# A decoder layer on one core: mLSTM queries and keys projected with stationary activations and turned by VectorE and moves, FOX columns as one run of seven groups

## The chip, the core and the metric

The kernel runs on one core of a Trainium2 chip. The metric is the device time of one launch in microseconds (us). Before the change it was 1252.22 us, the median of three runs between 1251.11 and 1255.26.

TensorE (PE) multiplies a stationary operand of up to 128 rows x 128 columns with a moving operand of up to 128 x 512 and accumulates into banks of 128 x 512 float32. VectorE (DVE) and ScalarE (ACT) evict and prepare, GpSimd (POOL) and SyncE (SP) issue transfers. Each engine works through its own queue in order.

## The reference, cut to what matters

One layer, batch 1, 256 tokens (S), model width 2048, in float32:

```python
h = rms_norm(x, mix_norm_g)
z = h @ w_in                    # 2048 x 7184: mq mk mv mo mi mf fq fk fv ff
ha = mlstm(mq, mk, mv, mi, mf)  # 4 heads of 256, then per-head norm, * sigmoid(mo)
hb = forgetting_attention(rms_norm(fq), rms_norm(fk), fv, log_sigmoid(ff))  # 8 heads of 128
x = x + concat([ha, hb]) @ w_out
x = x + (gelu(conv3(a)) * g) @ w_down      # a, g = split(rms_norm(x) @ w_up), width 5632
x = x + sigmoid(rms_norm(x) @ w_ple_gate) * (p @ w_ple_proj)
```

The change concerns the second line: the order in which the columns of `z` are computed, and for `mq` and `mk` which operand is stationary.

## The kernel before, in words

**Precision.** A float32 product is made of three: each operand is split into `hi`, its rounding to fp32r, and `lo`, the rest, and hi x hi, hi x lo and lo x hi are added. ACT casts `hi` (L282) and DVE subtracts `lo` (L284) for each block of weights.

**The stream.** `run_stream` walks a list of blocks. A block is one DMA of weights of up to 128 x 1024 elements, issued by SP (L267) three blocks ahead, its split on ACT and DVE also up to three blocks ahead (`AHEAD_SPLIT`), and a function that issues its matmuls on PE. After each block, `pull(2)` takes two steps from `side`, a queue of generators: norms, gates, attention heads, mLSTM scores. Steps are taken alternately from the first two jobs of the queue; those behind wait. `since(n, start)` lets a job wait until n blocks have passed. The framework orders the instructions of each engine by a schedule of its own that follows this order as priority, gives tiles of one tag their buffers, and sets the semaphores.

**Two kinds of groups.** `token_group` (L294 to L320) keeps the activations stationary: for each of 16 k tiles and each of two row tiles of 128 tokens it issues three matmuls with n weight columns moving (L313, L314, L315) into one bank per row tile. Its output has tokens on partitions. With n = 512, a block holds two k tiles, and so it does for each n down to 342. `wide_group` (L323 to L351) keeps the weights stationary: for each k tile and each of four column blocks of 128 it issues one matmul with 512 moving columns (`hi` and `lo` of the activations side by side, L345) and one with 256 (L346) into four banks. Its output is already transposed, with features on partitions; `merge` (L353) adds the two halves of a bank.

**The order of w_in.** FOX keys (2 groups of 512), FOX queries with the mLSTM gates (3 of 344), FOX values with the forget gates (3 of 344), then mLSTM queries and keys as two wide groups each, then values and output gate (2 token groups of 512 each), then `w_out`. The first group also loads and transposes `x` (`load_x`, `prep_x`).

**Squares.** Where token-major columns are needed as feature-major, `square` (L193) lets DVE transpose 32x32 squares, and `move` (L199) lets POOL issue 16 DMAs that put the squares into their places. The FOX queries and keys of each pair of heads go this way (`qk_squares`, tiles `qky` and `qkz`); a head then scales its part with an ACT operation (L567). The residual after `w_out` (`x2y`, `x2z`) and the up projection (`EZ`, `Y`) do the same.

**mLSTM queries and keys.** `qk_group` evicts each bank of a wide group with `merge` into `mqT` or `mkT` (ACT L354, DVE L355) and multiplies each pair by the row of 1/rms (`r1["b"]`, L628), which `rstd_rows` (L157) made with a PE transpose (L160), a copy and two DMAs. `mlstm_scores` multiplies `mkT` with `mqT` (L655, L658) once all FOX heads are taken; `mlstm_out` follows the second group of values, `mlstm_gate` the output gate.

**Buffers.** The token-major columns of FOX and mLSTM (`zbuf`) share three buffers of one tag. The transposed activations `hT`, `catT` (the mixers' outputs), `x2T`, `uA` and `x3T` are pairs of tiles (`Tiles`): 12 k tiles under the tag `aTa`, 4 under `aTb`, two buffers each. In the down projection (`run_units`) six blocks of `aTa` serve as extra `hi`, `lo` and sums (`w2`).

Of the kernel before, what the change touches and what calls it, by code (L numbers as in the profile page):

```python
# [9 lines left out]
F32 = mybir.dt.float32  # L10
F32R = mybir.dt.float32r
# [4 lines left out]
P = 128  # L16
S = 256
# [12 lines left out]
C_FK, C_FV = 5128, 6152  # L30
GATED = 1032
# [12 lines left out]
FRONT = 12  # L44
# [4 lines left out]
def layer_kernel(  # L49
# [19 lines left out]
    def bank(tag, name):  # L69
        return ps.tile([P, 512], F32, tag=tag, name=name)  # L70
# [85 lines left out]

    def rstd_rows(r, pool_):  # L157

        bk = bank("aux", "rstdT")
        pe.transpose(bk[:NT, :P], r, ident)  # L160
        rT = sm.tile([NT, P], F32, tag="rT", name="rT")
        dve.tensor_copy(rT, bk[:NT, :P])
        d = kp.tile([1, S], F32, tag="rstd", name="rstdd", bufs=2)
        pool.dma_start(out=d[0].rearrange("(t p) -> t p", p=P), in_=rT)
        rb = pool_.tile([P, S], F32, name="rb")
        pool.dma_start(out=rb, in_=d.broadcast_to([P, S]))
        return rb
# [155 lines left out]
    def wide_group(w, c0, actT, finish, tag, hold=0):  # L323

        st = {}
        parts = []
        blocks = []
        for k0 in range(0, KD, 2):  # L330
            def fn(hi, lo, k0=k0):
                if k0 == 0:
                    st["b"] = [bank(tag, f"wg{j}") for j in range(4)]
                parts.append((k0, hi, lo))
                if KD - 2 * (hold + 1) <= k0 < KD - 2:
                    return
                for j in range(4):
                    o = st["b"][j]
                    cols = slice(j * P, (j + 1) * P)
                    for kk, h, l in parts:  # L340
                        for i in range(2):
                            a = actT()[:, kk + i, :]
                            first = kk == 0 and i == 0
                            last = kk == KD - 2 and i == 1
                            pe.matmul(o, h[:, i, cols], a, start=first, stop=False)  # L345
                            pe.matmul(o[:, 256:512], l[:, i, cols], a[:, 0:256], start=False, stop=last)  # L346
                    if k0 == KD - 2:
                        finish(j, o)
                parts.clear()
            blocks.append((wsrc(w, k0, 2, c0, 512), fn, None, None, LO_SHIFT))  # L350
        return blocks  # L351

    def merge(dst, b):  # L353
        act.copy(dst, b[:, 256:512])  # L354
        dve.tensor_add(dst, b[:, 0:256], dst)  # L355

    class Tiles:


        def __init__(self, name):  # L360
            self.a = apool.tile([P, FRONT, 512], F32R, tag="aTa", name=name, bufs=2)
            self.b = apool.tile([P, KD - FRONT, 512], F32R, tag="aTb", name=name + "b", bufs=2)

        def __getitem__(self, idx):
            k = idx[1]
            if isinstance(k, slice):
                v, o = (self.a, 0) if k.stop <= FRONT else (self.b, FRONT)
                k = slice(k.start - o, k.stop - o)
            else:
                v, o = (self.a, 0) if k < FRONT else (self.b, FRONT)  # L370
                k -= o
            return v[(idx[0], k, *idx[2:])]

    def new_aT(name):
        return Tiles(name)
# [4 lines left out]
    with mixers:  # L380
# [16 lines left out]
        catT = new_aT("catT")  # L397
# [155 lines left out]
        taken = set()  # L553

        def fox_heads():
            def gen(heads):
                while "em" not in g:
                    yield
                zv = z["fv"]
                scale = FD ** -0.5  # L560
                for h in heads:
# [50 lines left out]
                    split_T(catT[:, 8 + h, :], ob[:, 0:256])  # L612
                    yield
# [5 lines left out]
        mqT = mp.tile([P, 8, S], F32, name="mqT")  # L619
        mkT = mp.tile([P, 8, S], F32, name="mkT")  # L620

        def qk_group(dstT, grp):
            def f(j, b):
                d = dstT[:, grp * 4 + j]
                merge(d, b)
                if j % 2 == 1:
                    d = dstT[:, grp * 4 + j - 1 : grp * 4 + j + 1]
                    dve.tensor_mul(d, d, r1["b"].unsqueeze(1).broadcast_to([P, 2, S]))  # L628
            return f

        WT = {}

        def mlstm_scores():
            def gen():
                while len(taken) < FH:
                    yield
# [4 lines left out]
                for h in range(MH):  # L641
# [12 lines left out]
                    for i in range(2):  # L654
                        pe.matmul(sb[:, 0:256], mkT[:, 2 * h + i, 0:128], mqT[:, 2 * h + i, :],  # L655
                                  start=i == 0, stop=i == 1)
                    for i in range(2):
                        pe.matmul(sb[:, 256:384], mkT[:, 2 * h + i, 128:256], mqT[:, 2 * h + i, 128:256],  # L658
                                  start=i == 0, stop=i == 1)
# [91 lines left out]

        for c in range(2):
            f = evac(get("fk"), c * 512, 512)
            kw = dict(prep=prep_x, load=load_x) if c == 0 else {}
            add(C_FK + c * 512, 512, after(f, lambda: fox_norm("fk", 0)) if c == 1 else f, **kw)
        for c in range(3):
            f = evac(get("fq"), c * 344, 344)
            add(C_MI + c * 344, 344, after(f, lambda: fox_norm("fq", 8)) if c == 2 else f)
        for c in range(3):
            f = evac(get("fv"), c * 344, 344)  # L760
            add(C_FV + c * 344, 344, after(f, gate_math, fox_heads) if c == 2 else f)
        for c in range(2):
            blocks.extend(wide_group(w_in, C_MQ + c * 512, lambda: hT, qk_group(mqT, c), "mm", 1))
        for c in range(2):
            f = qk_group(mkT, c)
            if c == 1:
                f = lambda j, b, f=f: (f(j, b), j == 3 and mlstm_scores())
            blocks.extend(wide_group(w_in, C_MK + c * 512, lambda: hT, f, "mm", 1))
# [48 lines left out]
    with tc.tile_pool(name="ffn", bufs=1) as fp:  # L817
# [98 lines left out]
        def new_raw(j, name):  # L916
# [58 lines left out]
        def run_units(us, first_late, gate):  # L975
            loaded = split = 0
            for i, u in enumerate(us):
                if i == first_late:
                    v = apool.tile([P, 6, BLK], F32R, tag="aTa", name="w2", bufs=2)
                    room.update(late=2, pT=1, e0=1, e1=1, ring=1)  # L980
                    late.update(gate=gate, free=i + LAST_UP + 1, hi=v[:, 0:2], lo=v[:, 2:4],
                                S=v[:, 4:6].rearrange("p b (i c) -> p b i c", c=256))
# [340 lines left out]
```

## Time and profile before

| what | value |
|---|---|
| median of three runs | 1252.22 us |
| the profiled execution | 1252.8 us |
| its span | 1251.1 us |
| granted PE clock, mean | 0.998 |
| PE, DVE, ACT, POOL busy | 1242.3, 829.6, 684.1, 211.4 us |
| w_in stage: wide groups | 147 to 249 us |

The profiled execution is one launch taken by the hardware profiler; its span runs from its first to its last instruction, and the 1.7 us around it belong to the launch. PE rows are matmuls, PEld rows the loads of the stationary operand, which overlap them. A record's line number (L345) is that of the kernel above; names are the program's tiles. A wait is put down to what came last.

### The profile page before, as it was taken

To read this page: it belongs to the slowest core of one execution; us is meant where nothing else is said; L and a number is where in the kernel's file an instruction comes from. 1 tells how busy PE (TensorE), PEld (TensorE's weight loads), DVE (VectorE), ACT (ScalarE), POOL (GpSimd) and SP (SyncE) were. 2 spreads that over 40 slices of the span, in tenths; PEclk is the share of its full clock that TensorE was granted. 3 is DMA by queue.
4 is the path that set the end of the run, shared out by engine and by line. 5 is a ranking of instruction groups with operands and counts; after the bars stand their busy time and mean duration, and the time that the engine had idled before them with its cause. 6 is when DMAs were issued, how large, how long until landed. Compare 5 with 4: busy or idle time off the path is not lost.

```text
span 1251.1 us, 16509 instructions
## 1 busy us (share of the span) xinstructions
PE 1242.3 (99%) x5890; PEld 1051.7 (84%) x5890; DVE 829.6 (66%) x1049; ACT 684.1 (55%) x962; POOL 211.4 (17%) x395
## 2 busy tenths in 40 slices
PE   8999999999999999999999999999999999999998
PEld 7899988888888888888888888888887888888887
DVE  5455567754565654765776676567669998898553
ACT  7655545645554454655565565556556555566542
POOL 2003034200304302112202211220220000050000
PEclk9999999999999999999999999999999999999999
DMA  8667776756667757678777867877798885786560
GB/s 249 175 191 194 217 210 187 207 152 173 197 187 213 224 188 216 207 227 240 229 227 216 252 219 222 242 233 228 221 293 278 283 288 194 261 263 230 174 217 35
DMA packets 133332, 270.74 MB, mean 216 GB/s; under 512 B 13991, under 2 KB 28961, under 8 KB 133249
## 3 DMA queue, kind: packets, MB, share of 16 engines
q1 hardware_dynamic: 119792, 245.99, 63.9%
q0 software_dynamic: 13072, 23.53, 6.6%
q8 instruction: 46, 0.75, 0.2%
q14 instruction: 37, 0.30, 0.1%
q10 hardware_dynamic: 385, 0.16, 0.0%
HBM read 246.02 MB, written 6.83 MB: 202 GB/s over the span
## 4 chain that ended last, share of the span: by engine, by line
PE 95%; DMA 2%; DVE 1%; ACT 1%; issue 0%; POOL 0%; SPq 0%; DVEq 0%; ACTq 0%; POOLq 0%
PE up L1257 13%; PE up L1256 13%; PE up L1258 13%; PE tg L314 10%; PE tg L313 10%; PE tg L315 10%; PE wg L345 5%; PE wg L346 2%; PE dnP L1018 1%; PE dnP L1019 1%; DMA EZ<-Y 1%; PE dnP L1017 1%; PE dn(0, 1)_8857 L1018 1%; PE dn(1, 0)_8861 L1019 1%; PE dn(1, 0)_8861 L1018 1%; PE dn(0, 1)_8857 L1017 1%
## 5 line engine op out<-in xcount | busy, mean ns | idle before, releaser
L970 DVE TENSOR_TENSOR lo<-raw,hi 128x1024 fp32r<-128x1024 f32 x222 | 271.0, 1222 | 177.4 <-ACT hi L969 177.0
L969 ACT CAST hi<-raw 128x1024 fp32r<-128x1024 f32 x222 | 233.2, 1051 | 250.0 <-DMA raw<-in_w_up_dram 102.3
L284 DVE TENSOR_TENSOR lo<-raw,hi 128x1024 fp32r<-128x1024 f32 (+2 forms) x161 | 178.8, 1116 | 148.9 <-ACT hi L282 148.6
L282 ACT CAST hi<-raw 128x1024 fp32r<-128x1024 f32 (+2 forms) x161 | 153.6, 960 | 149.3 <-PE tg L315 81.9
L1258 PE MATMUL up<-hi,x2T 128*128 128x512 f32 x528 | 205.5, 389 | 0.0
L1257 PE MATMUL up<-lo,x2T 128*128 128x512 f32 x528 | 205.4, 389 | 0.0
L1256 PE MATMUL up<-hi,x2T 128*128 128x512 f32 x528 | 204.8, 389 | 0.0
L199 POOL DMA_DIRECT2D EZ<-Y x176 | 93.1, 535 | 175.7 <-DVE Y L193 145.5
L1256 PEld LDWEIGHTS up<-hi,x2T 128*128 128x128 f32 x528 | 99.1, 188 | 20.6
L1257 PEld LDWEIGHTS up<-lo,x2T 128*128 128x128 f32 x528 | 99.1, 188 | 20.5
L1258 PEld LDWEIGHTS up<-hi,x2T 128*128 128x128 f32 x528 | 99.1, 188 | 20.5
L314 PE MATMUL tg<-lo,hT 128*128 128x512 f32 (+1 forms) x288 | 103.4, 359 | 0.0
L313 PE MATMUL tg<-hi,hT 128*128 128x512 f32 (+1 forms) x288 | 102.3, 360 | 0.0
L315 PE MATMUL tg<-hi,hT 128*128 128x512 f32 (+1 forms) x288 | 102.0, 355 | 0.0
L1257 PE MATMUL up<-lo,x2Tb 128*128 128x512 f32 x176 | 68.5, 389 | 0.0
L1258 PE MATMUL up<-hi,x2Tb 128*128 128x512 f32 x176 | 68.5, 389 | 0.0
L345 PE MATMUL wg<-hT,hi 128*128 128x512 f32 x192 | 67.6, 399 | 0.0
L1256 PE MATMUL up<-hi,x2Tb 128*128 128x512 f32 x176 | 65.2, 389 | 0.0
L315 PEld LDWEIGHTS tg<-hi,hT 128*128 128x128 f32 x288 | 54.4, 189 | 5.7
L314 PEld LDWEIGHTS tg<-lo,hT 128*128 128x128 f32 x288 | 54.4, 189 | 5.6
L313 PEld LDWEIGHTS tg<-hi,hT 128*128 128x128 f32 x288 | 54.0, 189 | 5.5
L346 PE MATMUL wg<-hT,lo 128*128 128x256 f32 x192 | 52.1, 284 | 0.0
(770 smaller groups left out, 2409.7 us busy)
## 6 DMA issues: line engine op xcount, KB each, us to landing
raw<-in_w_up_dram SPq DMA_DIRECT2D x176, 512.0 KB, 4.7
raw<-in_w_in_dram SPq DMA_DIRECT2D x79, 512.0 KB, 4.1
raw<-in_w_down_dram SPq DMA_DIRECT2D x44, 512.0 KB, 6.0
raw<-in_w_in_dram SPq DMA_DIRECT2D x48, 344.0 KB, 3.6
raw<-in_w_out_dram SPq DMA_DIRECT2D x32, 512.0 KB, 4.7
EZ<-Y POOLq DMA_DIRECT2D x176, 64.0 KB, 5.7
w2raw<-in_w_down_dram SPq DMA_DIRECT2D x20, 512.0 KB, 6.1
w<-sums SPq DMA_DIRECT2D x17, 512.0 KB, 5.9
```

Source lines behind the costliest of these rows:

```text
L199: pool.dma_start(out=c[32 * b : 32 * b + 32, a::4], in_=y[32 * a : 32 * a + 32, :, b])
L282: act.copy(hi, raw[:, :w])
L284: dve.tensor_sub(lo, raw[:, :w], f32(hi))
L313: pe.matmul(o, ah, hi[:, i, :], start=first, stop=False)
L314: pe.matmul(o, ah, lo[:, i, :], start=False, stop=False)
L315: pe.matmul(o, al, hi[:, i, :], start=False, stop=last)
L345: pe.matmul(o, h[:, i, cols], a, start=first, stop=False)
L969: act.copy(hi, raw)
L970: dve.tensor_sub(lo, raw, f32(hi))
L1256: pe.matmul(o, ah, hi[:, n], start=k == 0, stop=False)
L1257: pe.matmul(o, ah, lo[:, n], start=False, stop=False)
L1258: pe.matmul(o, al, hi[:, n], start=False, stop=k == KD - 1)
```

## The change

Five things change together.

1. `wide_group`, `merge` and `rstd_rows` go. `mq` and `mk` become token groups of 512 columns. Each row tile's bank is evicted by ACT with the scale 1/rms into `mz`, turned in squares by DVE into `my`, and moved by POOL: for queries straight into `mqT`, whose layout becomes [partition, group, 8 chunks, 128]; for keys into a `zbuf` (`z["mk"]`), from which ACT copies it, 7 blocks after the group's end at the earliest, into `mkT`. `mz` and `my` lie in `spare`, a buffer of the tag of `hT`'s first part.
2. The score products read `mqT` through `feature`: eight runs of 32 columns in place of 256 columns in a row.
3. The columns from the mLSTM gates to the FOX forget gates, 3088 side by side, are one run of groups of 512, five times 432 and 416; an eviction writes the parts of up to two of `fq`, `fk` and `fv`. Queries come first, then keys, then values.
4. `Tiles` has three parts of 8, 4 and 4 k tiles; `catT`'s parts are taken when first used. The extra blocks of the down projection come from two tags accordingly.
5. `mlstm_scores` also waits for both copies of keys, `mlstm_gate` also for the end of all FOX heads (`out_done`).

```diff
+FOX_WIDTHS = (512, 432, 432, 432, 432, 432, 416)
-FRONT = 12
+FRONT = (8, 4, 4)
...
-            r1["b"] = rstd_rows(r1["t"], mp)
-            yield
...
-        catT = new_aT("catT")
+        catT = new_aT("catT", late=True)
+        spare = apool.tile([P, FRONT[0] * 512], F32, tag="aT0", name="spare", bufs=2)
+        mz = spare[:, 0:1024].rearrange("p (t c) -> p t c", t=NT)
+        my = spare[:, 1024:2048].rearrange("p (t b c) -> p t b c", t=NT, b=4)
...
-        mqT = mp.tile([P, 8, S], F32, name="mqT")
+        mqT = mp.tile([P, 2, NT * 4, P], F32, name="mqT")
         mkT = mp.tile([P, 8, S], F32, name="mkT")
-        def qk_group(dstT, grp):
-            def f(j, b):
-                d = dstT[:, grp * 4 + j]
-                merge(d, b)
-                if j % 2 == 1:
-                    d = dstT[:, grp * 4 + j - 1 : grp * 4 + j + 1]
-                    dve.tensor_mul(d, d, r1["b"].unsqueeze(1).broadcast_to([P, 2, S]))
-            return f
+        mk_in = set()
+        def mk_columns(grp, start):
+            while not since(7, start):
+                yield
+            act.copy(mkT[:, 4 * grp : 4 * grp + 4].rearrange("p k (a j) -> p k a j", j=32),
+                     z["mk"][:, grp].rearrange("p a (k j) -> p k a j", j=32))
+            mk_in.add(grp)
+            yield
+        def qk_group(name, grp):
+            def f(t, b):
+                act.activation(mz[:, t], b, AF.Copy, scale=r1["t"][:, t : t + 1])
+                square(my, t, 0, mz[:, t])
+                if t < NT - 1:
+                    return
+                if name == "mq":
+                    move(my, mqT[:, grp])
+                    return
+                if grp == 0:
+                    z["mk"] = zbuf("mk").rearrange("p t c -> p (t c)")[:, 0:2048].rearrange("p (g a c) -> p g a c", g=2, c=P)
+                move(my, z["mk"][:, grp])
+                side.append(mk_columns(grp, done[0]))
+            return f
+        def feature(m, k, t0, t1):
+            return m[:, k // 4, 4 * t0 : 4 * t1, 32 * (k % 4) : 32 * (k % 4) + 32]
...
-                while len(taken) < FH:
+                while len(taken) < FH or len(mk_in) < 2:
...
-                        pe.matmul(sb[:, 0:256], mkT[:, 2 * h + i, 0:128], mqT[:, 2 * h + i, :],
+                        pe.matmul(sb[:, 0:256], mkT[:, 2 * h + i, 0:128], feature(mqT, 2 * h + i, 0, 2),
...
+                while len(out_done) < FH:
+                    yield
...
+        runs_ = (("fq", C_MI, GATED), ("fk", C_FK, 1024), ("fv", C_FV, GATED))
+        ready_at = {"fq": (lambda: fox_norm("fq", 8),), "fk": (lambda: fox_norm("fk", 0),), "fv": (gate_math, fox_heads)}
+        c0 = C_MI
+        for n in FOX_WIDTHS:
+            jobs = [j for name, o, w in runs_ if c0 < o + w <= c0 + n for j in ready_at[name]]
+            kw = dict(prep=prep_x, load=load_x) if c0 == C_MI else {}
+            add(c0, n, after(fox_evac(c0, n), *jobs), **kw)
+            c0 += n
         for c in range(2):
-            blocks.extend(wide_group(w_in, C_MQ + c * 512, lambda: hT, qk_group(mqT, c), "mm", 1))
+            add(C_MQ + c * 512, 512, qk_group("mq", c))
         for c in range(2):
+            add(C_MK + c * 512, 512, after(qk_group("mk", c), *([mlstm_scores] if c else [])))
...
-                    late[tag] = apool.tile([P, 2, BLK], F32, tag="aTb", name="w2raw", bufs=2)
+                    late[tag] = apool.tile([P, 2, BLK], F32, tag="aT2", name="w2raw", bufs=2)
...
-                    v = apool.tile([P, 6, BLK], F32R, tag="aTa", name="w2", bufs=2)
+                    v = apool.tile([P, 4, BLK], F32R, tag="aT0", name="w2", bufs=2)
+                    S2 = apool.tile([P, 2, BLK], F32R, tag="aT1", name="S2", bufs=2)
```

More of the change, by code (lines that the diff above doesn't have):

```diff
@@ L321, in token_group @@
         return blocks
[L323 to L351, printed above, removed]
@@ L377, in layer_kernel, with new_aT @@
+    def new_aT(name, late=False):
+        return Tiles(name, late)
     all_k = list(range(0, KD, 2))
@@ L551, in row @@
             pool.dma_start(out=t, in_=kept[name][h : h + 1].broadcast_to([P, S]))
-        taken = set()
+        taken, out_done = set(), set()
         def fox_heads():
+            zv = z["fv"]
             def gen(heads):
@@ L612, in gen @@
                     split_T(catT[:, 8 + h, :], ob[:, 0:256])
+                    out_done.add(h)
                     yield
```

68 lines of the change are left out of this document (25 added, 43 removed).

## The prediction, made before the run

> **What bounds the kernel now.** I read the profile's page first: how much of the span TensorE (PE) fills, at which clock, and what the chain that ended last is made of.
>
> ```profile
> span 1251.1 us, 16509 instructions
> ...
> PE 1242.3 (99%) x5890; PEld 1051.7 (84%) x5890; DVE 829.6 (66%) x1049; ACT 684.1 (55%) x962; POOL 211.4 (17%) x395
> ...
> PEclk9999999999999999999999999999999999999999
> ...
> PE 95%; DMA 2%; DVE 1%; ACT 1%; issue 0%; POOL 0%; SPq 0%; DVEq 0%; ACTq 0%; POOLq 0%
> ```
>
> PE is busy for 1242.3 of 1251.1 us, its clock is granted in full, and 95% of the chain is PE. But a busy PE need not be a PE without stalls, so the next view is the list of PE's waits, over the whole span (columns: waiter, what it waited for, us in total, times, longest).
>
> ```profile
> PE xT L149 <- DMA xs<-in_x_dram: 2.3, 1, 2.3
> PE dn(1, 0)_8007 L1017 <- ACT hi L969: 1.1, 1, 1.1
> PE warm L90 <- DVE ones L86: 1.1, 1, 1.1
> ```
>
> These are all of PE's waits, and none lies in the stage that the change touches: two are in the first 8 us and one is in the down projection. The table by stretches (busy us and instruction count of each engine, clock, DMA share, GB/s) shows that stage, the four wide groups of mLSTM queries and keys from 147 to 249 us, and its two neighbours:
>
> ```profile
> 147.00:249.00 102.00, 102.00 (x599) 90.08 (x599) 73.53 (x149) 56.93 (x114) 33.19 (x63) 1.00 0.69 203
> 249.00:348.00 99.00, 99.00 (x452) 82.47 (x451) 51.49 (x80) 48.80 (x72) 11.31 (x20) 1.00 0.60 174
> 900.00:960.00 60.00, 58.87 (x260) 48.44 (x259) 46.33 (x55) 35.10 (x41) 9.03 (x17) 1.00 0.84 277
> ```
>
> PE is busy throughout, with VectorE (DVE) at 73.5, ScalarE (ACT) at 56.9 and GpSimd (POOL) at 33.2 of 102 us. So what the change takes from or adds to the other engines is worth nothing as long as it stays covered, and what it takes from PE's own stream is worth its full time. The question is what PE's stream costs, matmul by matmul.
>
> **What one matmul costs.** A record of a matmul is longer than its place in the stream, since neighbours overlap; the price is the distance from start to start. Two pairs of rows of the chain give it (start, us, what): each pair is the same place in successive groups.
>
> ```profile
> 73.80 0.31 PE tg L313 x2
> ...
> 118.93 0.31 PE tg L313 x2
> ...
> 513.87 0.68 PE up L1256 x3
> ...
> 557.39 0.68 PE up L1256 x3
> ```
>
> From 513.87 to 557.39 lies one group of the up projection, 16 x 4 x 3 = 192 matmuls of 512 columns: 43.52 / 192 = 226.7 ns each. From 73.80 to 118.93 lie three FOX groups of 344 columns, 3 x 16 x 2 x 3 = 288 matmuls: 45.13 / 288 = 156.7 ns each. The line through both is 70.0 ns per 168 columns, or 0.4167 ns a column, plus **13.3 ns for each matmul**. A third shape tests it: the wide groups issue pairs, one matmul of 512 columns and one of 256. In the timeline of PE, twelve such pairs lie between these starts:
>
> ```profile
> 153.62 0.40 PE L345 MATMUL wg<-hT,hi 128*128 128x512 f32 x1
> ...
> 157.78 0.39 PE L345 MATMUL wg<-hT,hi 128*128 128x512 f32 x1
> ```
>
> That is 4.16 / 12 = 346.7 ns a pair; the line says 768 x 0.4167 + 2 x 13.3 = 346.7. So three points lie on one line, and group ends cost nothing on it (the 288 matmuls cross three of them).
>
> **The change, part by part.** First, the wide groups become token groups. Their count stands in the groups of PE (192 on the first twelve k tiles and 64 on the rest, so 256 pairs):
>
> ```profile
> L345 PE MATMUL wg<-hT,hi 128*128 128x512 f32 x192 | 67.6, 399 | 0.0
> ...
> L345 PE MATMUL wg<-hTb,hi 128*128 128x512 f32 x64 | 22.8, 398 | 0.0
> ```
>
> Before: 256 x 346.7 = 88.8 us. A token group takes 16 k tiles x 2 row tiles x 3 products of 512 columns, and four of them have 384 matmuls: 384 x 226.7 = 87.0 us. The streamed columns are the same, 196,608; 128 matmuls fewer make **-1.7 us**.
>
> Second, the FOX columns. Before: two groups of 512 and six of 344, 192 x 226.7 + 576 x 156.7 = 133.8 us. After: 512, five of 432 and one of 416, again 3088 columns: 96 x 226.7 + 480 x 193.3 + 96 x 186.7 = 132.5 us. 96 matmuls fewer make **-1.3 us**. The widths of 432 and 416 do not occur in the trace; they lie between 344 and 512, so their price is interpolated, between 156.7 and 226.7.
>
> Third, rstd_rows goes. Of it, PE held one transpose:
>
> ```profile
> 37.37 0.27 PE L160 MATMUL rstdT<-ident,rstd_mix 128*2 128x128 f32 x1
> 37.57 0.25 PE L111 MATMUL gT<-ident,vrows 42*128 42x42 f32 x1
> ```
>
> From its start to the next one's are 0.2 us: **-0.2 us**. The sum on PE is -1.7 - 1.3 - 0.2 = **-3.2 us**.
>
> The Trainium skill (TensorE: Matmul & The Clock Gate, section "Wait — 56ns, not 53.3ns?") puts the fixed cost of a warm matmul at about 2.5 ns. By that figure the 224 matmuls would be worth 0.6 us and the sum would be -0.8 us. This kernel's rows give 13.3 ns.
>
> Now what the other engines get in exchange. Rows of the groups for the same operations (busy us, mean ns of one):
>
> ```profile
> L193 DVE STREAM_TRANSPOSE x2y<-xs 128x512 f32<-128x512 f32 x6 | 4.0, 692 | 0.0
> ...
> L743 ACT ACTIVATE mv<-tg,rstd_mix 128x512 f32<-128x512 f32 x4 | 2.8, 690 | 3.3 <-PE tg L315 3.3
> ...
> L354 ACT COPY mkT<-wg 128x256 f32<-128x256 f32 x8 | 3.0, 369 | 3.9 <-PE wg L346 3.5
> ...
> L355 DVE TENSOR_TENSOR mkT<-wg,mkT 128x256 f32<-128x256 f32 x8 | 3.3, 414 | 0.0
> ...
> L628 DVE TENSOR_TENSOR mkT<-mkT,rb 128x512 f32<-128x512 f32 x4 | 2.8, 688 | 0.1
> ...
> L969 ACT CAST hi<-raw 128x1024 fp32r<-128x1024 f32 x222 | 233.2, 1051 | 250.0 <-DMA raw<-in_w_up_dram 102.3
> ...
> L199 POOL DMA_DIRECT2D qkz<-qky x48 | 25.4, 537 | 15.3 <-DVE qky L193 12.8 <-ACT hi L282 1.1 <-ACT em L535 1.0
> ```
>
> ACT loses 16 merge copies (5.9 us) and gets 8 scaled evictions of 0.69 us and two copies of 128x1024, which I take at the 1.05 us of a cast of that size: +1.7 us. DVE loses 16 adds and 8 multiplications (12.1 us) and gets 8 transposes (5.5 us): -6.6 us. POOL gets 4 x 16 DMA issues of 0.537 us: **+34.4 us**, 67.6 instead of 33.2 us of this stage. The DMA engines get 64 x 32 KB, 2.1 MB beside the 20.7 MB (102 us at 203 GB/s) that the stage moves; its share of 0.69 goes to some 0.76. All of this lies beside PE, so I cost it at nothing, but POOL has to be looked at closely: a group's move holds its queue for 16 x 0.537 = 8.6 us, and the FOX heads' own moves stand in the same queue. Their slack, from POOL's and ACT's timelines (start, us, line), with the median us from issue to landing last:
>
> ```profile
> 171.35 7.90 POOL L199 DMA_DIRECT2D qkz<-qky  x15 [0.31 <-issue]
> ...
> 193.41 8.45 POOL L199 DMA_DIRECT2D qkz<-qky  x16 [12.78 <-DVE qky L193]
> ...
> 215.11 8.58 POOL L199 DMA_DIRECT2D qkz<-qky  x16 [1.09 <-ACT hi L282]
> ```
> ```profile
> 189.71 1.71 ACT L567 ACTIVATE qk<-qkz,vT 128x256 f32<-128x256 f32 x4
> ...
> 211.81 1.71 ACT L567 ACTIVATE qk<-qkz,vT 128x256 f32<-128x256 f32 x4
> ...
> 232.60 1.31 ACT L567 ACTIVATE qk<-qkz,vT 128x256 f32<-128x256 f32 x3
> ```
> ```profile
> qkz<-qky POOLq DMA_DIRECT2D x64, 32.0 KB, 3.3
> ```
>
> The last issue plus 3.3 us is at 182.6, 205.2 and 227.0; the use is at 189.7, 211.8 and 232.6, so the slack is 7.1, 6.6 and 5.6 us. If a group's 8.6 us stand ahead each time, ACT stands still for 1.5, 2.0 and 3.0 us. What is queued behind it are the casts of the weight blocks, for which PE waits; but they run three blocks ahead of PE (AHEAD_SPLIT), 3 x 12 x 226.7 ns = 8.2 us. That ACT has this lead is seen in its waits: in this stage it waits for PE to free a buffer, not the other way round.
>
> ```profile
> ACT hi L282 <- PE wg L345: 15.5, 9, 2.7
> ```
>
> The other new waits: the transposes into `my` wait for the landing of the group before, which takes 8.6 to 17.2 + 3.3 us of the some 25 us between groups; `z["mk"]` needs the buffer of the FOX queries, whose last read precedes the issues at 215.1, while the third group's move begins near 222 us (below). By my count of the side queue the mLSTM scores come four blocks later than now and still before the second mv group ends, after which their first reader runs. The waits on `out_done` and on the late `catT` part come after that. If one of these covers goes, the FOX and mLSTM products, in PE's fixed order, are late next.
>
> One operation is not in the trace: the score products stream mqT in eight runs of 32 columns. From the starts of one head's products (the last row is the next matmul behind them):
>
> ```profile
> 261.57 1.02 PE L655 MATMUL msc<-mqT,mkT 128*128 128x256 f32 x4
> 262.43 0.61 PE L658 MATMUL msc<-mqT,mkT 128*128 128x128 f32 x4
> 262.80 0.48 PE L313 MATMUL tg<-hi,hT 128*128 128x512 f32 x1
> ```
>
> A head takes 1.23 us and all four 4.9 us. The bounds are nothing (a contiguous read can't be the slower one, so a gain is excluded) and a doubling, +4.9 us. I take nothing, as 128-byte runs are nearer to a contiguous read than to single elements.
>
> So the span goes from 1251.1 to 1247.9 us. The profiled execution took 1252.8 us, 1.7 more than its span and 0.6 above the median of 1252.22; from the median the **forecast is 1249.0 us**.
>
> **The rivals.** *The POOL queue delays the FOX heads (slower).* Four groups end some 25 us apart (102 / 4, less 0.4 each); the first three moves are ready near 172, 197 and 222 us (147 - 1.5 + n x 25.1, plus 1.4 for eviction and transpose). If the order of POOL's queue puts them ahead of the qkz moves ready at 171.35, 193.4 and 215.1, they hold it for 0.7, 3.7 and 7.1 us before their own 8.6. The overruns beyond the slack are then 2.2, 5.7 and 10.1 us. With the full lead of 8.2 us, 1.9 us reach PE; with a lead of one block (2.7 us) it is 0 + 3.0 + 7.4 = 10.4 us, and the time 1252.2 - 3.2 + 10.4 = **1259.4 us**. It decides where the lead falls under some 5 us. For it: POOL already waited 12.8 us at the head of its queue for one transpose. Against it: ACT's 15.5 us of waiting for PE.
>
> *The reads in runs cost double:* -3.2 + 4.9, **1253.9 us**; nothing in the profile speaks for it, as no such read is in it.
>
> *A matmul's fixed cost isn't saved,* so the change does not do what it says: 13.3 ns belongs to the shapes and only some 2.5 ns go with each matmul, 224 x 2.5 ns + 0.2 = 0.8 us, **1251.4 us**. Three points on one line speak against it. It is the figure of the Trainium skill named above.
>
> *The one late wait goes as well.* The slots of the down projection's extra parts are cut anew (eight k tiles, not twelve, must be read before the first is free), and the 1.1 us in which PE waits for ACT's cast at L1017 may vanish: **1247.9 us**. Against it: the cast waits in a queue of DVE work that stays.
>
> **How the numbers follow.** Chances: forecast 0.60, POOL queue 0.19, reads in runs 0.07, fixed cost 0.06, late wait 0.08. A difference of 0.3% (3.8 us) is about what a measurement of this kernel can tell from no change; it lies at 1248.5 and 1256.0 us, the forecast just inside. With three runs between 1251.1 and 1255.3, I give the forecast two parts in five below 1248.5: faster 0.24 + 0.07 = 0.31; slower 0.18, from the POOL queue alone; within 0.3% the rest, 0.51. The range reaches from 1246.8, under the late wait's 1247.9 by a run's scatter, to 1257.0, past the reads in runs and into the milder half of the POOL queue; some 0.05 lies below and 0.15 above.
>
> **What would show it.** In the changed profile: tg matmuls of 512 columns 226.7 ns apart in the query and key groups, those of 432 columns 193.3 ns apart; four groups in some 100 instead of 102 us; no PE wait in the first 440 us beyond the two at the start. Wrong would be: PE waiting for `qk`, `sc` or `msc`, or for hi casts behind L567 (POOL queue); the msc rows longer than 1.23 us a head (runs); start-to-start of 432 columns under 185 ns (fixed cost); no wait at L1017 (late wait). A time beyond 1257 with gap-free PE rows would mean that PE's stream itself became dearer, which no step here foresees.

## The result, and the profile after

The changed kernel takes a median of **1248.81 us** (20 runs, 1247.43 to 1253.28), the kernel before 1251.78 us in the runs taken beside it (20 runs, 1249.87 to 1255.26). The ratio is 0.998, with a 95% interval of 0.997 to 0.9989; the medians differ by 2.97 us. The forecast was a sum of -3.2 us and 1249.0 us.

The page of the changed kernel, with the lines that answer to those of before:

```profile
span 1246.5 us, 16075 instructions
...
PE 1238.5 (99%) x5665; PEld 1043.7 (84%) x5665; DVE 824.3 (66%) x1024; ACT 685.7 (55%) x950; POOL 245.0 (20%) x457
```

PE has 225 records fewer and is 3.8 us less busy. POOL has its 34 us more, and DVE its 5 us less. All of PE's waits in the changed kernel (what waits, for what, us in total, times, longest):

```profile
PE dn(1, 0)_7768 L1009 <- ACT hi L960: 1.2, 1, 1.2
PE warm L91 <- DVE ones L87: 1.1, 1, 1.1
PE xT L150 <- DMA xs<-in_x_dram: 0.9, 1, 0.9
```

They are the three of before, at the same three places. No new one came with the moves, and the late one of the down projection stayed. The stretch of the four query and key groups in the changed kernel (length, then busy us and count of PE, PEld, DVE, ACT and POOL, then clock, DMA share, GB/s):

```profile
146.00:246.00 100.00, 100.00 (x468) 83.13 (x467) 64.13 (x113) 53.95 (x90) 51.75 (x98) 1.00 0.76 213
```

PE is full, as before. POOL is busy for 51.75 of 100 us instead of 33.19 of 102, and DMA at 0.76 instead of 0.69.

**Where the time came from.** The span fell by 4.6 us, more than the 3.2 of the sum. To part the stream from the start, I take two places that the chains of before, of the changed kernel and of most variants share: the last pair of products of the same early k tile in the first group, and the first row of three of the up projection (start, us). Before has the second at 513.87, quoted above; its first, and both of the changed kernel:

```profile
30.73 0.45 PE tg L315 x2
```
```profile
28.73 0.45 PE tg L304 x2
...
508.74 0.68 PE up L1248 x3
```

From place to place it is 483.14 us before and 480.01 us after: -3.13 us. Not all of that was saved. A small transpose of weight vectors (`gT`) ran within the stretch before (37.57 in the prediction's rows, 0.18 us to the next product), and in the changed kernel it runs ahead of the first place, again for 0.18 us:

```profile
23.95 0.25 PE L112 MATMUL gT<-ident,vrows 42*128 42x42 f32 x1
```

So 0.18 us only moved out of the stretch, and the stream became **2.95 us** shorter. The first place itself is reached 2.0 us earlier, and by nothing that the change does. The first 14 us in stretches of 3.4 us, before and then after, show what:

```profile
6.80:10.20 3.40, 2.36 (x8) 2.07 (x9) 2.91 (x5) 2.23 (x5) 1.36 (x4) 0.62 1.03 277
10.20:13.60 3.40, 3.40 (x18) 2.70 (x17) 1.32 (x2) 1.72 (x7) 0.00 (x0) 0.88 1.06 389
```
```profile
6.80:10.20 3.40, 3.40 (x18) 2.77 (x18) 2.71 (x6) 3.00 (x8) 1.46 (x4) 1.00 1.06 317
```

In before's profiled execution PE waited 2.3 us for a part of `x` (1.4 us longer than in after's), and the granted clock was 0.62 and then 0.88 in the next two stretches. In after's the same wait was 0.9 us and the clock stayed at 1.00. Behind the second place the changed kernel takes 0.6 us longer (737.8 instead of 737.2), 0.5 of it after the last product, which is why the span gained 4.6 and not 5.1 us. The start is a matter of the execution and not of the kernel: among the 20 runs of the changed kernel, fourteen with a mean clock of 0.999 or 1.0 lie between 1247.4 and 1249.7 us, and six with 0.997 or 0.998 between 1251.1 and 1253.3. So the distance between two places is the better measure here; it reproduces to about 0.1 us (a later variant of the same stream, with two buffers, gave 480.10), while medians of 11 to 20 runs leave intervals of some 2 us.

### The profile page after: what moved, and what is told of

The parts are those of the page before. It is cut to its first block, busy times and chain, and to the rows that moved or that the text cites. A ratio compares the mean times of both kernels' runs of the same rounds, so it can differ in the third digit from the quotient of the medians.

```text
span 1246.5 us, 16075 instructions
## 1 busy us (share of the span) xinstructions
PE 1238.5 (99%) x5665; PEld 1043.7 (84%) x5665; DVE 824.3 (66%) x1024; ACT 685.7 (55%) x950; POOL 245.0 (20%) x457
## 4 chain that ended last, share of the span: by engine, by line
PE 92%; DMA 3%; issue 3%; DVE 1%; ACT 0%; POOL 0%; SPq 0%; DVEq 0%; ACTq 0%; POOLq 0%
PE tg L302 13%; PE tg L303 13%; PE tg L304 13%; PE up L1250 12%; PE up L1249 12%; PE up L1248 12%; DMA raw<-in_w_down_dram 2%; PE dnP L1010 1%; PE dnP L1011 1%; PE dnP L1009 1%; PE dn(1, 0)_8622 L1009 1%; PE dn(0, 0)_8614 L1009 1%; PE dn(1, 0)_8622 L1010 1%; PE dn(0, 0)_8614 L1011 1%; PE dn(0, 1)_8618 L1009 1%
## 5 line engine op out<-in xcount | busy, mean ns | idle before, releaser
L273 DVE TENSOR_TENSOR lo<-raw,hi 128x1024 fp32r<-128x1024 f32 (+3 forms) x153 | 177.8, 1163 | 154.6 <-ACT hi L271 154.2
L1250 PE MATMUL up<-hi,x2T 128*128 128x512 f32 x704 | 274.0, 389 | 0.0
L1249 PE MATMUL up<-lo,x2T 128*128 128x512 f32 x704 | 273.9, 389 | 0.0
L1248 PE MATMUL up<-hi,x2T 128*128 128x512 f32 x704 | 270.0, 389 | 0.0
L271 ACT CAST hi<-raw 128x1024 fp32r<-128x1024 f32 (+3 forms) x153 | 153.0, 1000 | 155.3 <-PE tg L304 116.4
L303 PE MATMUL tg<-lo,hT 128*128 128x512 f32 (+2 forms) x480 | 181.5, 378 | 0.0
L302 PE MATMUL tg<-hi,hT 128*128 128x512 f32 (+2 forms) x480 | 180.8, 382 | 0.0
L304 PE MATMUL tg<-hi,hT 128*128 128x512 f32 (+2 forms) x480 | 180.3, 377 | 0.0
L1248 PEld LDWEIGHTS up<-hi,x2T 128*128 128x128 f32 x704 | 132.1, 188 | 27.3
L1250 PEld LDWEIGHTS up<-hi,x2T 128*128 128x128 f32 x704 | 132.1, 188 | 27.3
L304 PEld LDWEIGHTS tg<-hi,hT 128*128 128x128 f32 x480 | 90.1, 188 | 12.5
L303 PEld LDWEIGHTS tg<-lo,hT 128*128 128x128 f32 x480 | 90.2, 188 | 11.8 <-DVE lo L273 0.4
L302 PEld LDWEIGHTS tg<-hi,hT 128*128 128x128 f32 x480 | 89.7, 188 | 11.8
L304 PE MATMUL tg<-hi,catT 128*128 128x512 f32 x128 | 49.9, 390 | 0.0
L302 PE MATMUL tg<-hi,catT 128*128 128x512 f32 x128 | 49.8, 391 | 0.0
L303 PE MATMUL tg<-lo,catT 128*128 128x512 f32 x128 | 49.8, 389 | 0.0
```

The costliest lines, as they stand in the source:

```text
L271: act.copy(hi, raw[:, :w])
L273: dve.tensor_sub(lo, raw[:, :w], f32(hi))
L302: pe.matmul(o, ah, hi[:, i, :], start=first, stop=False)
L303: pe.matmul(o, ah, lo[:, i, :], start=False, stop=False)
L304: pe.matmul(o, al, hi[:, i, :], start=False, stop=last)
L1248: pe.matmul(o, ah, hi[:, n], start=k == 0, stop=False)
```

## The experiments

My theory was that of the prediction: PE's stream is all that counts, each matmul saved is worth 13.3 ns, and everything that the other engines get is covered. The rivals: the matmul's fixed cost is another, or POOL's queue sets an end and is only just covered. All times are medians, and ratios stand against the kernel before in the same session.

**1 and 2: each half alone.** First the kernel before with only the FOX columns regrouped:

```diff
-        for c in range(2):
-            f = evac(get("fk"), c * 512, 512)
...
+        for n in FOX_WIDTHS:
...
+            add(c0, n, after(fox_evac(c0, n), *jobs), **kw)
```

> The kernel before with the FOX columns as one run of seven groups, and nothing else of the change. Theory (each matmul costs PE 13.3 ns beside 0.4167 ns a column, and nothing else of the change reaches PE): 96 matmuls fewer, -1.3 us against before, a ratio of 0.999; matmuls of 432 columns 193.3 ns apart. Rival (a matmul's fixed cost is not saved, only some 2.5 ns go with it): -0.2 us. Rival (the gain is all in the query and key groups): 0.

Then the changed kernel with the eight FOX groups of before, so that only queries and keys differ:

```diff
-        for n in FOX_WIDTHS:
...
+        for c in range(3):
+            f = evac(get("fq"), c * 344, 344)
+            add(C_MI + c * 344, 344, after(f, lambda: fox_norm("fq", 8)) if c == 2 else f)
...
```

> The changed kernel with the FOX columns in eight groups as before (keys, queries, values; 512 and 344 columns). Theory: 128 matmuls and one PE transpose fewer than before, -1.9 us against before, a ratio of 0.9985. Rival (fixed cost not saved): -0.5 us. Rival (all of the gain is in the FOX columns): 0.

Measured: FOX alone 1250.93 us, ratio 0.9995 (0.9986 to 1.0004), which decides nothing; queries and keys alone 1249.66 us, ratio 0.9984 (0.9975 to 0.9992), which excludes no gain. The same two places on the chains of the FOX variant and of the query and key variant:

```profile
28.73 0.45 PE tg L316 x2
...
511.04 0.68 PE up L1265 x3
```
```profile
31.25 0.45 PE tg L304 x2
...
512.12 0.68 PE up L1240 x3
```

From place to place 482.31 and 480.87 us, so -0.83 us for FOX and -2.27 us for queries and keys, or -2.09 without `gT`, which runs ahead of the first place here too (at 26.5 us; in the FOX variant at 35.0, within the stretch as before). Together -3.10, and both at once made -3.13: the halves simply add, as two parts of one full stream must.

Why FOX gave 0.83 and not 1.3 is in its new widths. PE's timeline of the changed kernel within a group of 432 columns:

```profile
111.65 0.35 PE L303 MATMUL tg<-lo,hT 128*128 128x432 f32 x1
...
114.75 0.35 PE L304 MATMUL tg<-hi,hT 128*128 128x432 f32 x1
```

Sixteen steps in 3.10 us are 193.8 ns against 193.3 on my line. The group of 416 has 83 steps in 15.70 us: 189.2 ns against 186.7. That is 480 x 0.5 + 96 x 2.5 ns = 0.5 us, the missing part.

**3: the FOX columns in twelve groups.** If each matmul carries 13.3 ns, 480 more must cost 6.4 us.

```diff
-FOX_WIDTHS = (512, 432, 432, 432, 432, 432, 416)
+FOX_WIDTHS = (512,) + 10 * (236,) + (216,)
```

> The changed kernel with the same 3088 FOX columns in twelve groups (512, ten of 236, one of 216): 480 matmuls more than the changed kernel, the same columns. Theory: 480 x 13.3 ns = +6.4 us against the changed kernel, so +3.4 us against before, a ratio of 1.003; matmuls of 236 columns 0.4167 x 236 + 13.3 = 111.7 ns apart. Rival (some 2.5 ns each): +1.2 us against the changed kernel, still 1.8 us faster than before. A second rival, that PE becomes bound by the loads of its stationary operand (188 ns records): 236-column matmuls well over 112 ns apart, up to 188, +43 us.

Measured: 1256.52 us, ratio 1.0039 (1.0026 to 1.0051). A fixed cost of 2.5 ns would have left the kernel faster than before; it is excluded. The chain, and PE's timeline within a group of 236 columns:

```profile
29.02 0.45 PE tg L304 x2
...
516.33 0.68 PE up L1248 x3
```
```profile
99.71 0.28 PE L302 MATMUL tg<-hi,hT 128*128 128x236 f32 x1
...
103.42 0.28 PE L302 MATMUL tg<-hi,hT 128*128 128x236 f32 x1
```

From place to place 487.31 us, 7.30 more than the changed kernel, or 15.2 ns for each matmul added. That fits the 13.3 loosely. The 33 steps between the two rows take 112.4 ns each, close to the 111.7 of the line. The group of 216 columns in the same timeline (94 steps, 10.49 us):

```profile
140.45 0.27 PE L302 MATMUL tg<-hi,hT 128*128 128x216 f32 x1
...
150.94 0.27 PE L303 MATMUL tg<-lo,hT 128*128 128x216 f32 x1
```

That is 111.6 ns, where the line says 103.3: below 236 columns a narrower matmul is hardly cheaper here. At 236 columns the line and this least step fall together, so the run by itself can't tell a cost of each matmul from a floor under narrow ones; against the 2.5 ns the stronger case is the queries and keys, all of 512 columns.

**4: wide groups cut further.** In the kernel before, each product of 512 columns in the wide groups is issued as two of 256. Columns, weights and banks stay; only 256 matmuls come on top.

```diff
-                            pe.matmul(o, h[:, i, cols], a, start=first, stop=False)
+                            pe.matmul(o[:, 0:256], h[:, i, cols], a[:, 0:256], start=first, stop=False)
+                            pe.matmul(o[:, 256:512], h[:, i, cols], a[:, 256:512], start=False, stop=False)
```

> The kernel before with each 512-column product of the wide groups issued as two of 256 columns into the halves of the same bank: 256 matmuls and loads of the stationary operand more, the same columns, the same results, nothing else changed. Theory (13.3 ns a matmul): +3.4 us against before, a ratio of 1.0027, 256-column products 120 ns apart. Rival (some 2.5 ns a matmul): +0.6 us. Second rival (loads of the stationary operand become the bound at 188 ns each): up to 768 x 188 ns instead of 88.8 us, +56 us.

Measured: 1252.89 us, ratio 1.0012 (1.0001 to 1.0023). The theory's 1.0027 lies outside, the 1.0005 of the rival inside. The chain and PE's timeline of this variant:

```profile
28.71 0.45 PE tg L315 x2
...
513.21 0.68 PE up L1257 x3
```
```profile
152.73 0.28 PE L345 MATMUL wg<-hT,hi 128*128 128x256 f32 x1
...
156.03 0.28 PE L346 MATMUL wg<-hT,hi 128*128 128x256 f32 x1
```

From place to place it is 484.50 us, 1.4 more than before. Twenty-eight steps in 3.30 us are 117.9 ns, three of them 353.6 ns, where the pair of before takes 346.7 to 347.4 over its longest stretches without a break (27 pairs from 232.00 us, 23 from 187.85). By the rows and by the places that is 5 to 7, some **6 ns for each matmul added**. So 13.3 ns is not a constant of every matmul. The line holds from 344 to 512 columns; in these wide groups the step at 256 columns is 2 ns under it. That is not because the two halves have the same stationary operand: from the first half at 152.73 to the second at 152.85, and on to the third product at 152.97 with another one, the steps are alike. Nor is it the width alone, since products of 256 columns in the last group of the changed kernel (`tl`, from 1238.92 to 1241.44) come 120.0 ns apart, on the line. What the fixed part hangs on isn't settled.

**5 to 7: twice the moves.** Each move into `mqT` and `z["mk"]` is issued twice (the second writes the same bytes), then those of the queries alone, then those of the keys alone. POOL gets 64, 32 and 32 issues more, 34.4 or 17.2 us.

```diff
                 if name == "mq":
-                    move(my, mqT[:, grp])
+                    for _ in range(2):
+                        move(my, mqT[:, grp])
                     return
...
-                move(my, z["mk"][:, grp])
+                for _ in range(2):
+                    move(my, z["mk"][:, grp])
```

> The changed kernel with each of the four moves of queries and keys issued twice, the second writing the same values to the same places: 64 DMA issues or 34.4 us more on POOL. Theory (the moves are covered, since the schedule places the FOX and mLSTM products where PE need not wait): the time of the changed kernel within 0.1%, no new wait of PE. Rival (the POOL queue is near its limit): PE waits for qk, sc or msc or for hi casts behind them, +5 to +15 us.

> The changed kernel with only the two moves of queries issued twice (17.2 us more on POOL). After the run with all four moves twice, the theory is a chain with a slack: moves, copies of keys, scores, values, gate of the first two heads; in the changed kernel the second head's norm factor is ready at 314 us and used at 323, so some 8 us of delay are free and what goes beyond reaches PE. The queries' second moves lie far ahead of the keys' (178 to 220 us against 242 to 290), so half of that run's delay of 61 us at most reaches the chain. Theory: between 0 and +15 us against the changed kernel, PE's waits, if any, at msc, hap or the catT products, none at qk or sc. Rival (ACT and DVE stand still behind late qkz data and the hi casts come late): waits at tg for hi.

> The changed kernel with only the two moves of keys issued twice (17.2 us more on POOL). Theory of the slack: the second copy of keys comes later by one extra move (8.6 us) if only the last one counts, by up to 30 if both do; beyond 8 us it reaches PE. So 0 to +15 us against the changed kernel, with the waits at msc, hap or the catT products. Rival (POOL's total load decides): the same time as with the queries' moves twice.

Measured: all four moves twice 1278.04 us, ratio 1.0209 (1.0196 to 1.0222); the queries' 1260.63, 1.0075 (1.0057 to 1.0093); the keys' 1269.78, 1.0142 (1.0127 to 1.0157). Against the changed kernel's 1248.81 these are +29.2, +11.8 and +21.0 us. The theory that POOL stays covered falls at once; more moves reach PE from here on, and more steeply than I had expected: the queries' +11.8 lies within the 0 to +15 us of the theory of the slack, the keys' +21.0 does not. The rival that POOL's total load decides falls as well, since two runs with the same load differ by 9 us. New waits of PE with all moves twice, with the queries' twice, and with the keys' twice:

```profile
PE hap L714 <- DVE mv L711: 11.3, 2, 7.6
PE tg L302 <- ACT spare L598: 3.7, 1, 3.7
PE msc L641 <- ACT mkT L591: 2.1, 1, 2.1
```
```profile
PE tg L302 <- ACT spare L598: 3.7, 1, 3.7
PE hap L713 <- DVE mv L710: 2.5, 2, 2.3
```
```profile
PE hap L713 <- DVE mv L710: 7.8, 1, 7.8
PE hap L713 <- ACT mv L679: 6.2, 1, 6.2
```

PE stands at the products that follow the mLSTM scores (`hap`), at the score products themselves (`msc`), or at a bank that ACT has yet to empty into `mz` (L598); in the first and third run also for 1.1 and 0.6 us at a piece of `catT`. Which cover was used up shows in ACT's timeline: the scaling of the last FOX pairs (L530) and the copies of the keys (L591), in the changed kernel and with all moves twice:

```profile
183.64 1.70 ACT L530 ACTIVATE qk<-qkz,vT 128x256 f32<-128x256 f32 x4
222.35 1.70 ACT L530 ACTIVATE qk<-qkz,vT 128x256 f32<-128x256 f32 x4
257.00 1.71 ACT L530 ACTIVATE qk<-qkz,vT 128x256 f32<-128x256 f32 x4
276.38 1.05 ACT L591 COPY mkT<-mk 128x1024 f32<-128x1024 f32 x1
295.76 1.05 ACT L591 COPY mkT<-mk 128x1024 f32<-128x1024 f32 x1
```
```profile
187.43 1.70 ACT L530 ACTIVATE qk<-qkz,vT 128x256 f32<-128x256 f32 x4
242.47 1.70 ACT L530 ACTIVATE qk<-qkz,vT 128x256 f32<-128x256 f32 x4
290.87 1.71 ACT L530 ACTIVATE qk<-qkz,vT 128x256 f32<-128x256 f32 x4
325.11 1.05 ACT L591 COPY mkT<-mk 128x1024 f32<-128x1024 f32 x1
357.69 1.04 ACT L591 COPY mkT<-mk 128x1024 f32<-128x1024 f32 x1
```

The delay grows from step to step: 3.8 us, all of it from a slower start (its first place is at 32.53 instead of 28.73), then 20.1, 33.9, 48.7 and 61.9 us. So with 34 us more on POOL the chain of heads, key copies and scores comes 58 us later. None of these rows shows idle time ahead of it (a bracket at the end of the row would name it): ACT does not stand at them, so I read them as coming late in its program's order. Nor is POOL full: ahead of its two groups of key moves it stands idle for 11.4 and 31.7 us, until DVE has turned their squares. The other two runs part the heads from the keys. With the queries' moves twice the last pairs are scaled at 241.06 and 287.76, nearly as late as with all four; with the keys' twice they are on time (222.46 and 257.11), and yet the copies run at 295.96 and 331.26. So late heads are one way to late copies and not the only one. PE's own order hides much of the delay: of 58 us PE waits for 18.5.

The rest of the price is the clock. In this variant PE is idle for 3.7 us from 247 to 345 and for 14.8 us from 345 to 436, 18.5 together, but the two places lie 27.7 us further apart than in the changed kernel (32.53 to 540.24, 507.71 us). The clock is at one half in three stretches between them (length, busy us and count of PE, clock, DMA share, GB/s). The first sets in within a wait of 3.73 us, the second at the end of one of 2.08, the third within one of 3.74 that one of 7.58 follows:

```profile
270.06:276.89 6.83, 5.20 (x12) 0.50 0.53 152
358.80:362.21 3.41, 3.41 (x10) 0.50 0.61 208
372.46:389.53 17.07, 7.72 (x22) 0.50 0.11 32
```

PE worked for 16.3 us in them at half the clock and lost half of that, 8.2 us, nearly all of the 9.2 that the idle time leaves.

**8 and 9: two buffers.** All four groups go through one `mz` and one `my`, so the second key group's transposes wait until the first's move has landed. I gave each group of a kind its own, in the free part of `spare`, and did the same with all moves twice.

```diff
-        mz = spare[:, 0:1024].rearrange("p (t c) -> p t c", t=NT)
-        my = spare[:, 1024:2048].rearrange("p (t b c) -> p t b c", t=NT, b=4)
+        mzs = [spare[:, o : o + 1024].rearrange("p (t c) -> p t c", t=NT) for o in (0, 2048)]
+        mys = [spare[:, o : o + 1024].rearrange("p (t b c) -> p t b c", t=NT, b=4) for o in (1024, 3072)]
...
+            mz, my = mzs[grp], mys[grp]
```

> The changed kernel with two sets of mz and my in the same spare tile, one for each group of queries and of keys by turns; nothing else changed. In the changed kernel the second key group's squares ran at 276.4 us, 33 us after their columns were evicted and 19 us after the last move that reads the buffer they overwrite was issued (253.2 us, some 4 us to landing). Theory (the single buffer strings the four moves one behind the other, and the schedule sets the squares late because of it): the second copy of keys comes 5 to 20 us earlier than 295.8 us; PE does not wait either way, so the time is that of the changed kernel within 0.1%. Rival (something else, as the FOX heads, sets the squares late): the copy at about 296 us again.

> Two sets of mz and my, and each of the four moves issued twice as in the earlier run (which took 1278.0 us with one set). Theory of the string (one buffer): with two sets the second copy of keys comes well before the 357.7 us of that run, and most of its +29 us goes: 1249 to 1262 us. Rival (POOL's load of 69 us of moves beside 34 us of FOX moves decides): 1272 us or more again.

Measured: 1248.49 us, ratio 0.9978 (0.9969 to 0.9986), the same as the changed kernel; and with the moves twice 1275.78 us, ratio 1.0191 (1.0175 to 1.0207). The last key move on POOL in the changed kernel, then with two buffers, and the two copies with two buffers (count, ns, from first to last):

```profile
284.01 2.64 POOL L188 DMA_DIRECT2D mk<-spare  x5 [0.15 <-issue]
```
```profile
254.95 3.15 POOL L188 DMA_DIRECT2D mk<-spare  x6 [0.88 <-DMA mk<-spare]
```
```profile
L591 ACT COPY mkT<-mk x2: 1052/1052/1052, 277.2 to 294.4; 128x1024 f32<-128x1024 f32 x2
```

The moves end 28.5 us earlier, and the copies come where they came before. So the one buffer is not what sets them, with or without doubled moves; my theory for these two runs fell. Two buffers did take away one thing: with the moves twice, PE's 3.7 us at L598 are gone, while `hap` still waits for 11.2 us and `mob`, the products of the scores with the values, now for 6.8. That leaves, for all four moves twice, the FOX heads' own moves, which share POOL's queue, and the queue of side jobs, in which copies and scores stand behind the heads; that is argued and not shown. In this variant the last pairs are scaled at 243.19 and 296.38 instead of 223.16 and 257.78. What sets the copies at 277 and 294 us when nothing is doubled stays open, and so does what two buffers would do for the keys' moves alone twice, where the heads are on time: that was not run.

**10: a longer warm-up.** To see whether the fall of the clock at the start makes the scatter, 14 instead of 9 warm-up products are issued, which fills the wait for `x`.

```diff
-    for _ in range(9):
+    for _ in range(14):
```

> The changed kernel with 14 instead of 9 warm-up products in front (some 2 us more of PE work before the first x arrives). In the profiled executions in which PE waited 2.0 to 2.3 us for the first x, the granted clock fell to 0.62 to 0.70 in the stretch from 6.8 to 10.2 us and to 0.80 to 0.88 in the next; where it waited 0.9 to 1.4 us, it stayed at 1.00. Theory: the scatter of the time between runs (1247.4 to 1253.3 us) comes from there; with PE busy until x arrives the clock stays up, the slow half of the runs goes, and the median falls by 0 to 1 us. Rival: x arrives before the longer warm-up ends and the start comes up to 1.5 us later.

Measured: 1250.35 us (12 runs, 1248.88 to 1251.79), ratio 0.9988 (0.998 to 0.9996). No run lies above 1251.8, where the changed kernel has three of 20 above 1252, but the fastest is 1.5 us later than its fastest. The late starts go, and the early ones seem to go with them: no gain.

## Why the prediction was right, point by point

- **PE's stream bounds the kernel, and nothing else does:** right. PE has the same three waits, and the change of the stream between the two places, -2.95 us, agrees with the 2.97 of the medians. The forecast of 1249.0 us missed by 0.2 us, less than the runs scatter. That it came so near is partly luck: the kernel before had 1251.78 us in these runs and not the 1252.22 that I started from, which more than made up for the 0.25 us missing from the gain.
- **Queries and keys, -1.7 and -0.2 for the transpose:** right in kind, short by 0.2; alone they gave -2.27 us between the places, of which 0.18 are `gT`, so -2.09. I traced the rest to no single row.
- **FOX, -1.3:** right in kind, 0.5 too large; alone it gave -0.83 us, because 432 and 416 columns cost 193.8 and 189.2 ns and not the interpolated 193.3 and 186.7. The two errors partly cancel, so the sum of -3.2 stands against -2.95.
- **13.3 ns for each matmul:** a good slope between 344 and 512 columns, where the change lies, and no constant. Splitting 512 into 256s cost 6 ns for each matmul added, twelve FOX groups 15.2. The rival that only 2.5 ns go with a matmul (1251.4 us) is excluded by the queries and keys alone (-2.09 us, where it gives -0.5), and the twelve groups alone would not have done it, because of the least step. In the wide groups 6 ns is nearer to the 2.5 than to 13.3.
- **Everything beside PE at nothing:** right for this change. My reason was only partly right. I let each FOX pair come some 22 us after the last, with 6 to 7 us of slack; in the changed kernel they are scaled at 183.64, 222.35 and 257.00, up to 24 us later than before. The third group's move begins at 242 and not at 222, and the scores run from 282 us instead of 261. ACT did not stand at any of this, nor PE; I read that as the program's order having been laid out for it. ACT's lead had even grown:

```profile
ACT hi L271 <- PE tg L304: 40.8, 26, 2.4
```

Between 140 and 260 us it waits 40.8 us for PE to free a buffer, where in the kernel before it was 15.5 at the wide groups and 2.0 at token groups.
- **POOL's queue, the rival on the slower side:** it did not come, but it is real. The doubled moves show that 17 us more of POOL's time cost 11.8 to 21.0 us. Where it would decide I had put into ACT's lead over PE; it decided in the mLSTM scores and what follows them. By which step the delay gets from POOL to there is shown only in part.
- **Reads in runs at nothing:** right. The score products of one head in the changed kernel, and the next head's:

```profile
281.97 1.02 PE L639 MATMUL msc<-mqT,mkT 128*128 128x256 f32 x4
282.83 0.61 PE L642 MATMUL msc<-mqT,mkT 128*128 128x128 f32 x4
283.27 1.03 PE L639 MATMUL msc<-mqT,mkT 128*128 128x256 f32 x4
```

Four products of 256 columns take 0.86 us from start to start, in eight runs of 32 columns as in one of 256 before (261.57 to 262.43). From head to head it is 1.30 us; the second head, which a token product follows at 284.50 as in the rows of before, takes 1.23 us as there.
- **The late wait may go:** it stayed, 1.2 instead of 1.1 us.
- **The profiled execution against the median:** I took the two to differ by a constant 0.6 us. Two us of before's execution came from its start, from a longer wait and the lower clock behind it, which not every execution has. It did no harm, since the medians of both kernels hold such starts.

## What to carry to other kernels

Where TensorE has no gaps, count its matmuls and price them start to start from rows of the same width; the sum then holds to a few tenths of a us, and two fixed places on the chain measure it better than the medians of twenty runs, once the work between them has been compared: a product that only moved past the first place looks like a gain. Before costing another engine's new work at nothing, double it once: here 34 us on GpSimd's queue were free and the next 34 cost 29 us, as the delays add up from job to job and the idle PE then loses its clock as well. Cover is a property of the order of the work, and the profile shows that it is there, not how much is left.

## What the runs showed of the hardware

- **The start.** PE's timeline before (transposes of `x`, the second row behind its wait), then the first products with all moves twice:

```profile
4.93 0.66 PE L149 MATMUL xT<-ident,xs 128*128 128x128 f32 x4
7.84 1.11 PE L149 MATMUL xT<-ident,xs 128*128 128x128 f32 x4 [2.25 <-DMA xs<-in_x_dram]
```
```profile
9.28 0.63 PE L303 MATMUL tg<-lo,hT 128*128 128x512 f32 x1
9.71 0.63 PE L302 MATMUL tg<-hi,hT 128*128 128x512 f32 x1
```

Behind a wait of 2.25 us the same four transposes took 1.11 instead of 0.66 us. The Trainium skill (TensorE: Matmul & The Clock Gate, section "HAM oscillation — how this bites in real kernels") says that idle gaps above some 3.4 us throttle the clock; here a shorter one was enough. With all moves twice the wait was only 1.4 us, and yet the products are 0.43 us apart, not 0.23, until about 14 us, while the clock column says 1.00. The transposes ahead of that wait had taken 1.11 us already, so the clock had not yet risen. So at the start the step of the products tells more than that column. The same page of the Trainium skill (section "What's actually happening") says that one kernel meets the end of its cold phase at different matmuls from run to run. The starts here agree: the transposes at some 5 us took 0.66 us in the execution of before and 1.11 in this one. The first place was reached between 28.7 and 32.5 us in the executions shown here, so the starts can make a good part of the 6 us over which the runs of the changed kernel scatter.
- **A short wait later on.** PE's one late wait, in the down projection, can cost the clock too, and need not. In the profiled execution with two buffers (1251.54 us, 3.05 above its median) the clock was 0.51 from 955.10 to 958.50 us, behind a wait of 1.43 us, and the products were 0.43 us apart. With the longer warm-up the same wait was 1.44 us and the clock from 956 to 960 us 1.00. So this wait can make another part of the scatter.
- With the moves twice, waits of 2.08 us and more in the middle of the kernel were followed by a clock of 0.50 for 3.4 to 17.1 us, by the rows shown above, and it was still 0.50 for 5.2 us after PE was full again at 384.3 us. A stall costs more than its length.
- Matmuls of 216 and 236 columns came at 111.6 and 112.4 ns, so that 20 columns less saved 0.8 ns, where from 344 to 512 columns the line gives 8.3: these products have a least step of some 111 ns. The score products of 128 columns are no faster: four of them take 0.44 us from start to start in the rows above (282.83 to 283.27).
